# Second ConvGLU of a two-layer diffusion backbone in the seven-product scheme, with block sums made by adding transfers

## The chip, the cores and the metric

The kernel runs on one core of a Trainium2 chip. The metric is the device time of one execution in microseconds. Five engines work side by side, each through its own instruction stream in order: PE (TensorE: matmuls into PSUM, with weight loads listed apart as PEld), DVE (VectorE), ACT (ScalarE), POOL (GpSimd) and SP (SyncE, which only issues transfers). They wait for one another by semaphores. 16 DMA engines move the data.

## The reference

512 latent tokens and 256 context tokens of width 1024 pass two layers: attention and a ConvGLU (both streams), then a gated recurrence (HGRN2) and a ConvGLU (latent stream only). All is float32. What the change is about is the last part, the second ConvGLU:

```python
D_MODEL = 1024; SEQ = 512; D_FF = 2816; CONV_W = 3

def dwconv3(u, w, b):
    up = jnp.pad(u, ((0, 0), (1, 1), (0, 0)))
    return up[:, :-2] * w[0] + up[:, 1:-1] * w[1] + up[:, 2:] * w[2] + b

def conv_glu(h, w_up, conv_w, conv_b, w_down):
    gate, val = jnp.split(h @ w_up, 2, axis=-1)
    return (jax.nn.silu(dwconv3(gate, conv_w, conv_b)) * val) @ w_down

# in each layer
hx2 = rms_norm(x, norm2_g[layer]) * (1.0 + sc2) + sh2
x = x + g2 * conv_glu(hx2, ffn_w_up[layer], ffn_conv_w[layer], ffn_conv_b[layer], ffn_w_down[layer])
```

## The kernel before

Features lie on the 128 partitions, tokens along the free dimension. The program runs, in this order: norm and modulation, attention, its output projection (`attn_out`), the first ConvGLU (`ffn` with l=0, 770 columns: 512 latent, 256 context, two for the shifts), the recurrence (`hgrn`), its output projection (`hgrn_out`), the second ConvGLU (`ffn` with l=1, 514 columns), and the transposed output.

**Split operands.** A float32 factor x is split in two: ACT rounds it to wh, DVE makes wl = x - wh. A product is three matmuls: wh with the high and the low part of the activations, wl with the high part. A weight is first loaded raw by a transfer that SP issues (tile `wr`, pool `wp`, two buffers of 2048 columns), then split into operand tiles `wh`, `wl` of 512 columns, taken in turn from several small pools (`operand`). The splits carry a high priority, so they run ahead as far as buffers allow.

**ConvGLU.** `ffn` walks over 22 feature tiles `ft` of 128. `up(ft)` computes gate and value, runs the three-tap convolution, SiLU and the product on DVE and ACT, and keeps the split result `g`. After a round of tiles (`ROUNDS`), a down projection adds their part to the eight output tiles of x, one pair `dp` at a time. One tile of the next round is computed ahead of the down projection. The norm's factor R per token is applied to the output of the up projection, so it may come late; its row sums pass PE (`nss`), POOL (`rs`, the inverse root) and PE again (`nR`).

**Two forms of the up projection.** The first ConvGLU uses seven products (`load_pair`, `gate_pair`): the weights of a tile form a 2x2 matrix of blocks (a11, a12: first and second half of the 1024 inputs for the gate; a21, a22: the same for the value), the activations another (b11 to b22: input halves by column halves, made by `halves` and `combos` into the seven sets `hs`). Seven products of 4 k each with sums of blocks take the place of eight. DVE makes the four sums of weight blocks (L136) before the seven splits; POOL multiplies the value half by R. PSUM tiles pZ, pY and pV collect the products. ACT copies intermediate states of Z and V, DVE adds them. The second ConvGLU uses the plain form (`load_w`, `gate_plain`): four splits, 96 matmuls of 256 or 258 columns into `pd`, four evictions on DVE (L912). Its one set of split activations `hn` is made tile by tile in `hgrn_out` (`scaled`).

**What sets the order.** The code is written straight through; a list scheduler places each engine's instructions by priority and by its own estimate of readiness. The tile framework adds the semaphore waits. Each engine then runs its list in order.

## Time and profile before

| | us |
|---|---|
| three runs | 1875.34, 1877.10, 1877.72 (median 1877.1) |
| the profiled execution | 1872.88, span 1871.1 from first to last instruction |
| attention and its output projection | to about 428 |
| first ConvGLU | about 428 to 1003 |
| recurrence | about 1003 to 1412 |
| `hgrn_out` | about 1412 to 1481 |
| second ConvGLU and output | about 1481 to 1871 |

The stages are read from the first and last matmuls of each tile name. In rows of groups, `out<-in` names the tiles, then partitions x elements, the count after x, busy us and mean ns of one, and the idle time of the engine just before with what ended it. Clock is the TensorE clock that was granted, 1 being full.

### The profile page before, as it was taken

How to read it: one execution, taken by the hardware profiler on the slowest of the kernel's cores; microseconds unless marked ns; L12 is line 12 of the kernel's file. 1: busy time of each engine (PE TensorE's matmuls, PEld its weight loads, DVE VectorE, ACT ScalarE, POOL GpSimd, SP SyncE). 2: the span in 40 equal slices, each digit the busy share in tenths (PEclk: the TensorE clock that was granted, in tenths of full speed). 3: DMA queues.
4: the chain of work that ended last, by engine and by line, in shares of the span. 5: the costliest groups of instructions: out<-in, count | busy, mean ns of one | idle time of the engine just before them, and what ended most of it. 6: DMA issues, size and time to landing. Idle time of an engine off the chain costs nothing.

```text
span 1871.1 us, 32302 instructions
## 1 busy us (share of the span) xinstructions
PE 1801.3 (96%) x13326; PEld 1576.9 (84%) x13326; DVE 1214.1 (65%) x2243; ACT 754.7 (40%) x1478; POOL 247.4 (13%) x233
## 2 busy tenths in 40 slices
PE   6999999998999999999998999999998999999998
PEld 4976786787888888989887888988886799899997
DVE  5575667466867686766777676777676655455462
ACT  4354555465534252434354333333332443233332
POOL 1233333103201000101013101111110200000000
PEclk9999999998999999999998999999999999999999
DMA  9204104232333333233313212122220332333321
GB/s 309 66 23 158 47 24 169 68 102 68 124 113 102 113 124 113 91 113 124 113 61 90 58 35 58 35 57 58 57 69 24 90 91 91 90 96 96 92 82 65
DMA packets 204416, 166.44 MB, mean 89 GB/s; under 512 B 5149, under 2 KB 198254, under 8 KB 199150
## 3 DMA queue, kind: packets, MB, share of 16 engines
q1 hardware_dynamic: 196608, 160.47, 27.8%
q10 hardware_dynamic: 7662, 3.92, 0.7%
q8 instruction: 105, 1.72, 0.4%
q14 instruction: 41, 0.34, 0.1%
HBM read 162.27 MB, written 2.10 MB: 88 GB/s over the span
## 4 chain that ended last, share of the span: by engine, by line
PE 87%; DVE 5%; DMA 4%; issue 2%; ACT 1%; POOL 1%; SPq 0%; ACTq 0%; POOLq 0%; DVEq 0%
PE dn L170 15%; PE pd L170 13%; PE pZ L188 8%; PE pf L170 8%; PE pV L188 4%; PE pjq L598 4%; PE pv L170 4%; PE ao L170 4%; PE ho L170 3%; PE pq L170 3%; PE pv L824 2%; PE pt L816 2%; PE ada L309 2%; PE pY L188 2%; PE pgate L170 2%; PE kv L598 2%
## 5 line engine op out<-in xcount | busy, mean ns | idle before, releaser
L117 ACT ACTIVATE wh<-wr 128x512 fp32r<-128x512 f32 (+1 forms) x320 | 193.0, 618 | 452.3 <-DMA wr<-in_ffn_w_up 74.8
L118 DVE TENSOR_TENSOR wl<-wr,wh 128x512 fp32r<-128x512 f32 (+1 forms) x320 | 223.6, 705 | 140.3 <-ACT wh L117 138.3
L170 PE MATMUL dn<-g,wh 128*128 128x512 f32 (+1 forms) x1056 | 263.3, 357 | 2.2 <-ACT g L995 2.2
L170 PE MATMUL pd<-hn,wh 128*128 128x256 f32 (+1 forms) x1408 | 227.3, 284 | 0.9 <-issue 0.9
L170 PEld LDWEIGHTS dn<-g,wh 128*128 128x128 f32 x1056 | 175.4, 189 | 32.7 <-ACT g L995 2.8
L170 PEld LDWEIGHTS pd<-hn,wh 128*128 128x128 f32 x1408 | 194.2, 190 | 2.5 <-issue 2.3
L188 PE MATMUL pZ<-hs,wh 128*128 128x386 f32 x704 | 185.2, 345 | 3.0 <-ACT wh L140 1.5
L170 PE MATMUL dn<-g,wl 128*128 128x512 f32 (+1 forms) x528 | 159.4, 356 | 0.0
L140 ACT ACTIVATE wh<-wr 128x512 fp32r<-128x512 f32 x132 | 81.6, 628 | 167.9 <-DMA wr<-in_ffn_w_up 47.4
L170 PE MATMUL pd<-hn,wl 128*128 128x256 f32 x704 | 141.8, 283 | 0.0
L188 PEld LDWEIGHTS pZ<-hs,wh 128*128 128x128 f32 x704 | 128.0, 190 | 15.7 <-ACT wh L140 4.4
L141 DVE TENSOR_TENSOR wl<-wr,wh 128x512 fp32r<-128x512 f32 x132 | 94.0, 717 | 53.6 <-ACT wh L140 53.5
L170 PE MATMUL pf<-hn,wh 128*128 128x512 f32 (+1 forms) x512 | 119.3, 349 | 9.7 <-DVE xc L1023 8.8
L188 PE MATMUL pZ<-hs,wl 128*128 128x386 f32 x352 | 119.4, 343 | 2.2 <-DVE wl L141 2.2
L926 POOL TENSOR_TENSOR gg<-gg,R 128x772 f32<-128x772 f32 x22 | 53.9, 2449 | 458.3 <-DVE gg L925 446.6
L170 PEld LDWEIGHTS pd<-hn,wl 128*128 128x128 f32 x704 | 109.0, 190 | 0.0
L1023 DVE SCALAR_TENSOR_TENSOR xl<-dn,mod,xl 128x512 f32<-128x512 f32 x72 | 53.9, 748 | 73.7 <-PE dn L170 73.6
L170 PEld LDWEIGHTS dn<-g,wl 128*128 128x128 f32 x528 | 87.4, 188 | 14.8
L170 PEld LDWEIGHTS pf<-hn,wh 128*128 128x128 f32 x512 | 80.9, 192 | 22.5 <-ACT wh L117 9.1
L188 PE MATMUL pV<-hs,wh 128*128 128x386 f32 x352 | 92.2, 341 | 5.0 <-ACT hs L392 5.0
L598 PE MATMUL pjq<-wh,hn 128*128 128x256 f32 x384 | 77.8, 291 | 0.0
L188 PEld LDWEIGHTS pZ<-hs,wl 128*128 128x128 f32 x352 | 66.7, 190 | 6.6 <-DVE gg L925 3.4
(299 smaller groups left out, 3807.1 us busy)
## 6 DMA issues: line engine op xcount, KB each, us to landing
wr<-in_ffn_w_up SPq DMA_DIRECT2D x88, 512.0 KB, 5.1
wada<-in_ada_w SPq DMA_DIRECT2D x40, 1024.0 KB, 4.8
wr<-in_hgrn_w_in SPq DMA_DIRECT2D x40, 512.0 KB, 4.2
ar<-in_ada_w SPq DMA_DIRECT2D x32, 256.0 KB, 7.1
wr<-in_ffn_w_down SPq DMA_DIRECT2D x16, 512.0 KB, 4.1
wr<-in_ffn_w_down SPq DMA_DIRECT2D x8, 896.0 KB, 4.7
wr<-in_attn_w_in SPq DMA_DIRECT2D x6, 1024.0 KB, 8.1
wr<-in_attn_w_out SPq DMA_DIRECT2D x8, 512.0 KB, 4.9
```

What stands on the lines that cost most here:

```text
L117: nc.scalar.activation(wh, src, AF.Copy)
L118: nc.vector.tensor_tensor(wl, src, f(wh), op=ALU.subtract)
L140: nc.scalar.activation(ops[i][0], src, AF.Copy)
L141: nc.vector.tensor_tensor(ops[i][1], src, f(ops[i][0]), op=ALU.subtract)
L170: nc.tensor.matmul(o, lhsT=wt, rhs=at[:, t0:t0 + o.shape[1]], start=(first and n == 0 and i == 0), stop=(last and n == len(ks) - 1 and i = ...
L188: self.nc.tensor.matmul(ps, lhsT=wt, rhs=at, start=(first and k == 0 and i == 0), stop=(k == nk - 1 and i == 2), skip_group_check=not first)
L309: nc.tensor.matmul(ps[32 * j:32 * j + 32, 0:512], lhsT=self.cs[:, k, :], rhs=raw[:, j * 512:(j + 1) * 512], start=(k == 0), stop=(k == KT ...
L598: nc.tensor.matmul(out, lhsT=x, rhs=y[:, wk], start=(start and k == 0 and j == 0), stop=(stop and k == KT - 1 and j == 2))
L816: nc.tensor.transpose(pt[:, j * P:(j + 1) * P], pr[j][:, b * P:(b + 1) * P], self.ident)
L824: nc.tensor.matmul(pv[a * HD:(a + 1) * HD, 0:256], lhsT=V[:, tl, g, :], rhs=pT[:, a * 256:(a + 1) * 256], start=(b == 0), stop=(b == len(t ...
L926: times = lambda eng, o, x, y: eng.tensor_tensor(o, x, y, op=ALU.mult)
L1023: nc.vector.scalar_tensor_tensor(x[:, d], o, self.modc(l, v, 5, d), x[:, d], op0=ALU.mult, op1=ALU.add)
```

## The change

- **Blocks.** Raw weights are loaded in blocks of 512 columns (256 KB, one transfer each; `block`) from eight buffers, instead of 2048 columns from two. This concerns all weights and the conditioning matrix (`ada_steps`). Down weights come as 128 columns each instead of 256.
- **Seven products in the second ConvGLU.** `gate_plain` goes; `gate_pair` serves both. `hgrn_out` builds the seven sets by `halves` and `combos`; the last two of each set are made after all output tiles.
- **Sums by transfers.** For the second ConvGLU no engine makes the sums of weight blocks. Seven blocks are loaded per tile (some twice or three times), and POOL issues five transfers per tile from one block to another that add to what is there (L151 of the new program): first s1 += a22, s3 += a11, s4 += a11, then s2 += s1, s4 += s1. So that all sums are additions, signs move into `combos` (scale -1) and into `gate_pair` (copies with scale -1, subtractions). This sign change reaches the first ConvGLU too, whose sums stay on DVE.
- **Buffers.** A second pool of eight blocks (`wrB`) is opened for the second ConvGLU, 16 in all. The turn of operand pools changes to ten pairs there; `gpB` has 7 buffers for 9. R is multiplied on DVE instead of POOL there.
- **Rounds** of the second ConvGLU are 6, 6, 5, 5 for 8, 7, 7.

```diff
--- before.py
+++ after.py
...
-ROUNDS = ((3, 4, 4, 4, 3, 4), (8, 7, 7))
+ROUNDS = ((3, 4, 4, 4, 3, 4), (6, 6, 5, 5))
...
-    def load_raw(self, parts):
-        raw = self.wp.tile([P, 2048], F32, tag="wr", name="wr")
-        n = 0
+    def block(self, src):
+        nk, m = src.shape[1:]
+        pool = self.wps[0]
+        self.wps = self.wps[1:] + self.wps[:1]
+        raw = pool.tile([P, 512], F32, tag="wr", name="wr")[:, 0:nk * m]
+        self.nc.sync.dma_start(out=raw.rearrange("p (k m) -> p k m", m=m), in_=src)
+        return raw
+    def split(self, src, op=None):
+        wh, wl = op or (t[:, 0:src.shape[1]] for t in self.operand())
+        with self.tc.high_priority(offset=W_AHEAD):
+            self.nc.scalar.activation(wh, src, AF.Copy)
+            self.nc.vector.tensor_tensor(wl, src, f(wh), op=ALU.subtract)
+        return wh, wl
+    def load_w(self, parts):
+        out = []
         for src in parts:
             nk, m = src.shape[1:]
...
+            step = 512 // m
+            blocks = [self.block(src[:, k:min(k + step, nk)]) for k in range(0, nk, step)]
+            ops = [self.split(b) for b in blocks]
+            out += [ops[i:i + 2] for i in range(0, len(ops), 2)]
         return out
-    def load_pair(self, parts, tmp):
...
+    def load_pair(self, parts, tmp, lat_only):
+        nc = self.nc
+        p1, p2 = parts
+        low, high = slice(0, 4), slice(4, 8)
+        ops = [self.operand() for _ in range(7)]
+        def total(o, x, y):
+            nc.vector.tensor_tensor(o, x, y, op=ALU.add)
...
-        with self.tc.high_priority(offset=W_AHEAD):
-            parts(0, a11)
-            parts(1, a12)
-            total(s1, a21, a22, ALU.add)
-            s3 = total(a21, a11, a21, ALU.subtract)
-            s2 = total(a11, s1, a11, ALU.subtract)
-            parts(3, s2)
-            parts(6, s3)
-            parts(2, s1)
-            parts(5, a22)
-            s4 = total(a12, a12, s2, ALU.subtract)
-            parts(4, s4)
+        if not lat_only:
+            a11, a12, a21, a22 = (self.block(p[:, k]) for p in parts for k in (low, high))
+            s1 = tmp.tile([P, 512], F32, tag="s1", name="s1")
+            with self.tc.high_priority(offset=W_AHEAD):
+                self.split(a11, ops[0])
+                self.split(a12, ops[1])
+                total(s1, a21, a22)
+                s3 = total(a21, a11, a21)
+                s2 = total(a11, s1, a11)
+                for i, src in ((3, s2), (6, s3), (2, s1), (5, a22)):
+                    self.split(src, ops[i])
+                self.split(total(a12, a12, s2), ops[4])
+            return ops
+        a11, a22, s1, s3, a12, s2, s4 = (self.block(p[:, k]) for p, k in
+                                         ((p1, low), (p2, high), (p2, low), (p2, low), (p1, high), (p1, low), (p1, high)))
+        with self.tc.high_priority(offset=2 * W_AHEAD):
+            for o, x in ((s1, a22), (s3, a11), (s4, a11), (s2, s1), (s4, s1)):
+                nc.gpsimd.dma_start(out=o, in_=x, accum_op=ALU.add)
+        for i, src in ((0, a11), (1, a12), (3, s2), (6, s3), (2, s1), (5, a22), (4, s4)):
+            self.split(src, ops[i])
         return ops
...
-            raw = self.wp.tile([P, 2048], F32, tag="wr", name="wada")
-            nc.sync.dma_start(out=raw, in_=self.a["ada_w"][l, k * P:(k + 1) * P, r * 2048:(r + 1) * 2048])
+            raw = []
...
-                nc.tensor.matmul(ps[32 * j:32 * j + 32, 0:512], lhsT=self.cs[:, k, :], rhs=raw[:, j * 512:(j + 1) * 512],
+                raw.append(self.wp.tile([P, 512], F32, tag="wr", name="wada"))
+                nc.sync.dma_start(out=raw[j], in_=self.a["ada_w"][l, k * P:(k + 1) * P, r * 2048 + j * 512:r * 2048 + j * 512 + 512])
+            for j in range(4):
+                nc.tensor.matmul(ps[32 * j:32 * j + 32, 0:512], lhsT=self.cs[:, k, :], rhs=raw[j],
...
-        def put(i, src):
-            nc.scalar.activation(hs[i][:, 0, kk], src, AF.Copy)
-            nc.vector.tensor_tensor(hs[i][:, 1, kk], src, f(hs[i][:, 0, kk]), op=ALU.subtract)
+        def put(i, src, sign=1.0):
+            nc.scalar.activation(hs[i][:, 0, kk], src, AF.Copy, scale=sign)
+            if sign > 0:
+                nc.vector.tensor_tensor(hs[i][:, 1, kk], src, f(hs[i][:, 0, kk]), op=ALU.subtract)
+            else:
+                nc.vector.scalar_tensor_tensor(hs[i][:, 1, kk], src, sign, f(hs[i][:, 0, kk]), op0=ALU.mult, op1=ALU.subtract)
...
-            put(5, diff(b21, t4, t3))
+            put(5, diff(b21, t3, t4))
...
         put(0, b11)
...
         t1 = diff(b12, b12, b11)
-        put(2, t1)
+        put(2, t1, -1.0)
...
-        put(3, t2)
+        put(3, t2, -1.0)
...
-        put(5, diff(b21, b21, t2))
+        put(5, diff(b21, t2, b21))
...
-        if R.shape[1] > TW:
-            nc.vector.memset(R[:, TW:], sh)
+        if R.shape[1] > TW or lat_only:
+            nc.vector.memset(R[:, C0 if lat_only else TW:], sh)
...
-    def gate_plain(self, ft, ops, hn, G, gg, R, rows, half, tmp, bank):
...
-    def gate_pair(self, ft, ops, hs, G, gg, R, rows, half, tmp, bank):
...
+    def gate_pair(self, ft, ops, hs, G, gg, R, rows, lat_only, tmp, bank):
+        nc = self.nc
+        half = hs[0].shape[3]
...
+        less = lambda o, x: nc.vector.tensor_tensor(o, o, x, op=ALU.subtract)
...
         prod(0, Z, True)
...
         prod(1, Y, True)
         add(g[0], t0, Y)
         prod(3, Z)
-        nc.scalar.activation(g[2], Z, AF.Copy)
+        nc.scalar.activation(g[2], Z, AF.Copy, scale=-1.0)
...
         if ft == 0:
             prod(2, Z)
...
             prod(4, Z)
             prod(6, V, True)
-            nc.scalar.activation(g[3], V, AF.Copy)
+            nc.scalar.activation(g[3], V, AF.Copy, scale=-1.0)
             prod(5, V)
         else:
             prod(6, V, True)
-            nc.scalar.activation(g[3], V, AF.Copy)
+            nc.scalar.activation(g[3], V, AF.Copy, scale=-1.0)
             prod(2, Z)
             nc.scalar.activation(t2, Z, AF.Copy)
             prod(5, V)
             prod(4, Z)
-        add(g[3], g[3], t2)
-        add(g[2], g[2], V)
+        less(g[3], t2)
+        less(g[2], V)
...
         times(nc.vector, g[0], g[0], R[:, 0:half])
         times(nc.vector, g[1], Z, R[:, half:])
-        times(nc.gpsimd, gg, gg, R)
+        times(nc.vector if lat_only else nc.gpsimd, gg, gg, R)
...
-        half = C0 // 2 if lat_only else hs[0].shape[3]
+        half = hs[0].shape[3]
...
         def up(ft):
-            ws_ = [self.wcols(wup, ft * P, P), self.wcols(wup, DFF + ft * P, P)]
-            ops = self.load_w(ws_) if lat_only else self.load_pair(ws_, tmp)
+            ops = self.load_pair([self.wcols(wup, ft * P, P), self.wcols(wup, DFF + ft * P, P)], tmp, lat_only)
...
-            (self.gate_plain if lat_only else self.gate_pair)(ft, ops, hs, G, gg, R, rows, half, tmp, bank)
+            self.gate_pair(ft, ops, hs, G, gg, R, rows, lat_only, tmp, bank)
...
             for dp in range(KT // 2):
-                w = self.load_w([wdn[f0 * P:(f0 + nf) * P, dp * 256:dp * 256 + 256].rearrange("(k p) m -> p k m", p=P)], True)
+                w = self.load_w([wdn[f0 * P:(f0 + nf) * P, d * P:d * P + P].rearrange("(k p) m -> p k m", p=P)
+                                 for d in (2 * dp, 2 * dp + 1)])
...
-    def hgrn_out(self, part, hn, acc, tmp, pj):
-        nc = self.nc
-        self.shifts(1, 1, hn)
+    def hgrn_out(self, part, hs, acc, tmp, pj):
+        nc = self.nc
...
+        some = []
...
                 self.add_gated(1, 2, d, pd, True)
+            some.append(self.combos(self.halves(1, 1, dp, 258, True, tmp, ("y0", "y1"), 4), dp, hs))
+            next(some[-1])
...
-                self.scaled(1, 1, d, hn, True)
...
+        for rest in some:
+            for _ in rest:
+                pass
...
-        self.wp = self.pool(top, "wp", 2)
+        self.wp = self.pool(top, "wp", 8)
...
+        self.wps = [self.wp]
...
-        self.wsp.append(self.pool(top, "wsC", 2))
+        wsC = self.pool(top, "wsC", 2)
+        self.wsp = [self.ws0, wsC, self.ws0]
...
-        self.wsp.append(self.pool(top, "wsD", 2, right=True))
+        wsD = self.pool(top, "wsD", 2, right=True)
+        self.wsp = [self.ws0, wsC, self.ws0, wsD]
...
-        hn = self.hn_tile(hc, "hn3", C0)
+        hs1 = hc.tile([P, 7, 2, 4, 258], F32R, tag="hs", name="hs3")
+        hs = [hs1[:, i] for i in range(7)]
...
-        self.hgrn_out(part, hn, acc, ot, pj)
+        self.hgrn_out(part, hs, acc, ot, pj)
...
-        R = Rp.tile([P, C0], F32, tag="R", name="R2")
+        R = Rp.tile([P, 516], F32, tag="R", name="R2")
...
-        gp = self.pool(es, "gpB", 9)
-        self.wsp.append(self.pool(es, "wsE", 2))
+        gp = self.pool(es, "gpB", 7)
+        self.wps = [self.wp, self.pool(es, "wrB", 8)]
+        self.wsp = [self.ws0, wsC, self.ws0, wsD, self.pool(es, "wsE", 2)]
...
-        self.ffn(1, hn, R, rows, True, tmp, acp, bk, gp, done1)
+        self.ffn(1, hs, R, rows, True, tmp, acp, bk, gp, done1)
```

At the start of the second ConvGLU, POOL's list ended like this before (`acc2`: sum of squares for the norm; `rs`: inverse root; numbers tell buffers apart):

```order
L515 TENSOR_TENSOR acc2_15106<-acc2_15106,sq_15222 128x512 [waits Activation_49,Pool_49]
L515 TENSOR_TENSOR acc2_15106<-acc2_15106,sq_15297 128x512 [waits Activation_49,Pool_49]
L515 TENSOR_TENSOR acc2_15106<-acc2_15106,sq_15302 128x512 [waits Activation_49,Pool_49]
L429 TENSOR_TENSOR rs_15405<-rv_15406,mh_66 128x4 [waits DVE_49]
L1449 UNCONDITIONAL_BRANCH
```

and now (`wr<-wr`: an adding transfer; for the first tile a11 is 16000, a22 16002, s1 16004, s3 16006, a12 16008, s2 16010, s4 16012; 161xx is the second tile):

```order
L518 TENSOR_TENSOR acc2_15666<-acc2_15666,sq_15932 128x512 [waits Activation_49,Pool_49]
L432 TENSOR_TENSOR rs_16084<-rv_16085,mh_66 128x4 [waits DVE_49]
L151 DMA wr_16004<-wr_16002 128x512 [waits DMAHW0_49,DMAHW1_49,DVE_49,Pool_49]
L151 DMA wr_16006<-wr_16000 128x512 [waits DMAHW1_49]
L151 DMA wr_16182<-wr_16176 128x512 [waits DMAHW4_49,DMAHW3_49]
L151 DMA wr_16180<-wr_16178 128x512 [waits DMAHW4_49]
L151 DMA wr_16010<-wr_16004 128x512 [waits DMAHW2_49,DMASW1_49]
L151 DMA wr_16012<-wr_16004 128x512 [waits DMASW0_49]
```

The first tile's s1 and s3 come right behind `rs`; its second level (s2, s4) waits for transfers (DMASW) and stands behind two sums of the second tile.

SP's list at the same place before (raw weights of 512 KB a transfer):

```order
L95 DMA wr_15329<-in_ffn_w_up 128x8x128 [waits DMAHW6_49,DMAHW5_49,DVE_49]
L95 DMA wr_15329<-in_ffn_w_up 128x8x128
L95 DMA wr_15481<-in_ffn_w_up 128x8x128 [waits DMAHW7_49,DMAHW0_49,DVE_49]
L95 DMA wr_15481<-in_ffn_w_up 128x8x128
L95 DMA wr_15618<-in_ffn_w_up 128x8x128 [waits DMAHW2_49,DMAHW1_49,DVE_49]
```

and now:

```order
L96 DMA wr_16336<-in_ffn_w_up 128x4x128 [waits DMAHW6_49,DVE_49]
L96 DMA wr_16340<-in_ffn_w_up 128x4x128 [waits DMAHW7_49,DMAHW1_49,DVE_49]
L96 DMA wr_16002<-in_ffn_w_up 128x4x128 [waits DVE_49,DMAHW0_49,PE_49,Pool_49]
L96 DMA wr_16006<-in_ffn_w_up 128x4x128
L96 DMA wr_16010<-in_ffn_w_up 128x4x128 [waits DMAHW2_49]
L96 DMA wr_16176<-in_ffn_w_up 128x4x128 [waits DMAHW3_49]
```

The blocks from the new pool (16002, 16006, 16010 of the first tile) come behind two of the third tile, and the first of them waits for PE and POOL.

On PE the piece after the output projection read before:

```order
L170 MATMUL pd<-hn_15102,wl 128x256
L170 MATMUL pd<-hn_15102,wl 128x258
L524 MATMUL nss<-cst,acc_15106 128x2 x4
L533 MATMUL nR<-dg,cst 128x512
L170 MATMUL pd<-hn_15102,wh 128x256
```

and now:

```order
L186 MATMUL pY<-hs_15662,wh 128x258 x2
L186 MATMUL pY<-hs_15662,wl 128x258
L527 MATMUL nss<-cst,acc_15666 128x2 x4
L186 MATMUL pV<-hs_15662,wh 128x258 x2
L536 MATMUL nR<-dg,cst 128x512
L186 MATMUL pZ<-hs_15662,wh 128x258 x2
```

`nss` stood behind 48 matmuls of the first tile and now stands behind its products 0 and 1 (24 matmuls); two matmuls on a sum of weight blocks stand ahead of `nR`.

More of the change, by code (lines that the diff above doesn't have):

```diff
@@ L96, in load_raw @@
-            n += nk * m
-        return raw, n
-    def load_w(self, parts, cols=False):
-        nc = self.nc
-        raw, n = self.load_raw(parts)
-        nk, m = parts[0].shape[1:]
-        out = []
-        for lo in range(0, m, P) if cols else range(0, n, 1024):
-            size = nk * P if cols else min(1024, n - lo)
-            ops = []
-            for i in range(0, size, 512):
-                c = min(512, size - i)
-                wh, wl = (t[:, 0:c] for t in self.operand())
-                src = raw[:, lo + i:lo + i + c]
-                with self.tc.high_priority(offset=W_AHEAD):
-                    if cols:
-                        src = ap(raw[:, i // P * m + lo:i // P * m + lo + 1], 0, (m, c // P), (1, P))
-                        wh, wl = (t.rearrange("p (k c) -> p k c", c=P) for t in (wh, wl))
-                    nc.scalar.activation(wh, src, AF.Copy)
-                    nc.vector.tensor_tensor(wl, src, f(wh), op=ALU.subtract)
-                    if cols:
-                        wh, wl = (t.rearrange("p k c -> p (k c)") for t in (wh, wl))
-                ops.append((wh, wl))
-            out.append(ops)
-        return out
@@ L125, in load_pair @@
-    def load_pair(self, parts, tmp):
-        nc = self.nc
-        raw, n = self.load_raw(parts)
-        q = n // 4
-        a11, a12, a21, a22 = (raw[:, i * q:(i + 1) * q] for i in range(4))
-        s1 = tmp.tile([P, 512], F32, tag="s1", name="s1")[:, 0:q]
-        ops = [tuple(t[:, 0:q] for t in self.operand()) for _ in range(7)]
-        def total(o, x, y, op):
-            nc.vector.tensor_tensor(o, x, y, op=op)
-            return o
-        def parts(i, src):
-            nc.scalar.activation(ops[i][0], src, AF.Copy)
-            nc.vector.tensor_tensor(ops[i][1], src, f(ops[i][0]), op=ALU.subtract)
-        with self.tc.high_priority(offset=W_AHEAD):
-            parts(0, a11)
-            parts(1, a12)
-            total(s1, a21, a22, ALU.add)
-            s3 = total(a21, a11, a21, ALU.subtract)
-            s2 = total(a11, s1, a11, ALU.subtract)
-            parts(3, s2)
-            parts(6, s3)
-            parts(2, s1)
-            parts(5, a22)
-            s4 = total(a12, a12, s2, ALU.subtract)
-            parts(4, s4)
+            step = 512 // m
```

13 lines of the change are left out of this document (1 added, 12 removed).

## The prediction

> **What bounds the kernel now.** I read the page's busy times first, then the chain of waits, then a table by stage, then PE's waits.
>
> ```profile
> PE 1801.3 (96%) x13326; PEld 1576.9 (84%) x13326; DVE 1214.1 (65%) x2243; ACT 754.7 (40%) x1478; POOL 247.4 (13%) x233
> PE 87%; DVE 5%; DMA 4%; issue 2%; ACT 1%; POOL 1%; SPq 0%; ACTq 0%; POOLq 0%; DVEq 0%
> ```
>
> PE is busy nearly all the time, and it is also the chain. For the second ConvGLU, where most of the change lies, the chain in order of time reads:
>
> ```profile
> 1483.57 4.62 issue
> ...
> 1490.12 2.04 PE nR L533 x2
> 1492.16 98.39 PE pd L170 x816
> 1590.55 44.23 PE dn L170 x192
> 1634.78 80.50 PE pd L170 x672
> 1715.28 38.60 PE dn L170 x168
> 1753.88 69.00 PE pd L170 x576
> ```
>
> `pd` is the up projection, `dn` the down projection. From 1492 to 1823 us nothing but matmuls stands in the chain: this stage is bound by the number and width of matmuls. An up matmul costs 98.39/816 = 0.1206 us (256 or 258 columns), a down matmul 44.23/192 = 0.2304 us (512 columns). The table by stage gives the other engines (columns: PE, PEld, DVE, ACT, POOL busy us; clock; DMA share; GB/s), for an up stretch, a down stretch and the whole first ConvGLU:
>
> ```profile
> 1492.16:1590.55 98.39, 98.39 (x818) 98.39 (x817) 59.44 (x120) 40.13 (x62) 0.00 (x0) 0.99 0.29 87
> 1590.55:1634.78 44.23, 44.23 (x195) 36.13 (x194) 17.35 (x27) 10.48 (x18) 0.00 (x0) 1.00 0.33 95
> 428.00:1003.00 575.00, 553.57 (x3124) 496.58 (x3116) 419.77 (x697) 243.30 (x442) 80.31 (x48) 0.99 0.34 106
> ```
>
> The first ConvGLU already uses the seven products; there DVE is busy for 419.77/575 = 73% and PE hardly waits for the splits:
>
> ```profile
> PE pZ L188 <- DVE wl L141: 2.2, 3, 1.6
> PE pZ L188 <- ACT wh L140: 1.5, 4, 0.4
> ```
>
> **The products.** Before, a feature tile takes 2 outputs x 8 k x 3 x 2 column halves = 96 matmuls; after, 7 products x 4 k x 3 = 84 of 258 columns. Over 22 tiles 264 matmuls fall away: 264 x 0.1206 = 31.8 us. The price at exactly this width and with one use of each weight is not in the trace; the nearest row besides is the first ConvGLU's product of 386 columns:
>
> ```profile
> 646.60 2.13 PE pZ L188 x12
> ```
>
> That is 0.1775 us each. A line through it and the 512-column matmul gives 0.1238 at 258 columns, so the saving would be 2112 x 0.1206 - 1848 x 0.1238 = 25.9 us. I take 31.8, since `pd` has the same width; 25.9 is the lower end. The down matmuls stay (528 of 512 columns). Rounds of 6, 6, 5, 5 for 8, 7, 7 add eight evictions on DVE,
>
> ```profile
> L1023 DVE SCALAR_TENSOR_TENSOR xl<-dn,mod,xl 128x512 f32<-128x512 f32 x24 | 18.0, 750 | 48.1 <-PE dn L170 48.1
> ```
>
> 0.75 us each, under down stretches in which DVE is busy for 17.35 of 44.23 us: nothing.
>
> **DVE and ACT in an up stretch.** One tile must now fit under 84 x 0.1206 = 10.13 us of PE. The means of single instructions, second ConvGLU:
>
> ```profile
> L118 DVE TENSOR_TENSOR wl<-wr,wh 128x512 fp32r<-128x512 f32 x112 | 76.8, 687 | 70.5 <-ACT wh L117 70.3
> L989 DVE SCALAR_TENSOR_TENSOR u<-G,par,u 128x512 f32<-128x512 f32 x22 | 16.5, 752 | 0.8
> L992 DVE SCALAR_TENSOR_TENSOR gg<-gg,u 128x512 f32<-128x512 f32 x22 | 16.4, 747 | 0.0
> L996 DVE TENSOR_TENSOR g<-gg,g 128x512 fp32r<-128x512 f32 x22 | 15.2, 693 | 15.4 <-ACT g L995 15.4
> L912 DVE TENSOR_TENSOR G<-pd,R 128x258 f32<-128x258 f32 x22 | 9.2, 418 | 0.0
> L985 DVE TENSOR_SCALAR cb<-G,wsum,par 128x1 f32<-128x1 f32 x22 | 5.9, 267 | 0.0
> L983 DVE COPY G<-G 128x1 f32<-128x1 f32 x22 | 3.3, 149 | 0.0
> L117 ACT ACTIVATE wh<-wr 128x512 fp32r<-128x512 f32 x111 | 68.2, 630 | 159.4 <-DMA wr<-in_ffn_w_up 69.4 <-PE pd L170 37.2 <-PE dn L170 26.3
> ```
>
> DVE after: 7 splits x 0.687, five operations of 258 columns x 0.418, one of 516 at 0.69, two u at 0.75, then 0.747, 0.693, 0.267 and 0.149: 10.95 us. The same sum for today's tile (4 splits, four evictions, the same tail) is 7.78 us, or 66 us for the 8.5 tiles of the first up stretch, where DVE was really busy for 59.44: means overlap by a tenth. So 10.95 means about 9.9 busy, 97% of an up stretch. Over a whole round the down stretch gives relief (ten operand pairs let splits run ahead): 22 x 9.9 plus four times some 14 in the down stretches (8 evictions, 16 splits a round) is 80% of 222.9 + 121.6 us of PE, against the 73% that cost the first ConvGLU next to nothing. ACT goes from 4 to 7 splits (4.4 us) and gets four copies of 258 columns; its tail stays, so it keeps room. Bounds: 0 below, 22 x (10.95 - 10.13) = 18 above; I take 4, nearer to the first ConvGLU's rows.
>
> **The seam into the second ConvGLU.** `hgrn_out` now builds seven operand sets instead of one. Under the output matmuls there is room; exposed is what follows the last one. The rows of POOL, SP and PE shown with the change tell the rest. POOL had nothing behind `rs`; now the first tile's sums stand behind it, the second level waits for the first to land, and later tiles' sums are queued behind that wait. On SP the first tile's blocks from the new pool (16002, 16006, 16010) wait for PE, since the pool takes the place of buffers that the last output matmul reads, and the loads behind them wait too. The old seam:
>
> ```profile
> 1479.67 0.40 PE L170 MATMUL ho<-oh,wl 128*128 128x512 f32 x1
> 1480.96 0.72 PE L170 MATMUL pd<-hn,wh 128*128 128x256 f32 x4 [0.89 <-issue]
> ...
> 1486.77 0.95 PE L524 MATMUL nss<-cst,acc 128*128 128x2 f32 x8
> 1488.23 1.02 POOL L429 TENSOR_TENSOR rs<-rv,mh 128x4 f32<-128x4 f32 x1 [4.66 <-DVE rv L428]
> ```
>
> ```profile
> wr<-in_ffn_w_up SPq DMA_DIRECT2D x88, 512.0 KB, 5.1
> ar<-in_ada_w SPq DMA_DIRECT2D x32, 256.0 KB, 7.1
> xs<-in_x ACTq DMA_DIRECT2D x8, 256.0 KB, 2.7
> ```
>
> New: eviction 0.75, ACT's scaled copy, one split, so products 0 and 1 (24 matmuls, no sums) end near 1485; `nss` and `rs` until 1487.5; level one lands 2.7 later (a 256 KB transfer's lower row), level two 2.7 after that, split 0.63 + 0.69: 1494.2. By then today's kernel has done 48 + 17 matmuls, the new one 26: 39 x 0.1206 = 4.7 us lost. With 7.1 for each landing it is 13.5. I take 8, since all blocks of two tiles arrive at once there. If the loads were early, nothing but the 2 us before product 0 would show.
>
> **Transfers in the stage.** In finer blocks of 256 KB the same bytes move for the rest of the program; PE waits there for DMA only at the start (first row), so I count nothing. In the second ConvGLU a tile loads 7 blocks for 4 and makes 5 sums. Slices of 1.5 us from 1740 to 1800:
>
> ```profile
> PE ada L275 <- DMA ar<-in_ada_w: 10.8, 3, 9.0
> ...
> DMA  5000399000089400004982000079600000970000
> GB/s 126 0 0 0 89 330 270 20 0 0 9 253 323 114 0 0 0 0 119 265 240 86 0 5 0 0 215 330 165 0 0 0 0 27 307 277 0 0 11 0
> ```
>
> A full slice moves about 330 GB/s, so 7 + 2 blocks of 0.262 MB take 7.1 us. A sum moves at least two times 0.262 MB (1.6 us), at most three (2.4 us: two reads and a write, none overlapping): 7.9 to 11.9 us for five. PE needs 10.13 + 24 x 0.2304 = 15.7 us per tile; with 15.0 the transfers fit, with 19.0 not. I take the lower: reads and writes of one copy overlap in every load of this trace.
>
> The Trainium skill, "Collectives: The Full Stack", § The bandwidth ceiling, says that an add in the DMA path costs two source reads on one ring and therefore runs at half a copy's rate, not slower for the adding itself; by it an adding transfer takes twice a copy, the 1.6 us above, and no run here shows it yet.
>
> **Sum.** 1872.9 (profiled execution, span 1871.1 and 1.8 around it) - 31.8 + 4 + 8 = 1853.1. The median of the runs lies 4.2 us above the profiled one: 1857.
>
> **Rivals.**
> *All hidden* (15%): the seam costs 2 and DVE nothing: 1872.9 - 31.8 + 2 + 4.2 = 1847. For it: PE's few waits in the first ConvGLU. Against: the order of POOL above.
> *DVE paces the up stretches* (10%): 18 for the 4: 1871. For it: 97%; against: the 73% row.
> *The adding transfers pace it, slower* (20%): 19.0 us a tile for 15.7 is 22 x 3.3 = 73 us more: 1930. It decides from 1.7 us a sum on, and the gain is gone at 1.9. Against: a copy's overlap; for: nothing in this trace has ever added in flight.
> *POOL's issuing slows DVE* (5%): POOL and DVE do hinder one another here (start us, us).
>
> ```profile
> 1457.09 4.69 POOL L515 TENSOR_TENSOR acc<-acc,sq 128x512 f32<-128x512 f32 x3 [11.41 <-ACT sq L513]
> 1453.67 0.68 DVE L118 TENSOR_TENSOR wl<-wr,wh 128x512 fp32r<-128x512 f32 x1
> 1458.92 1.72 DVE L118 TENSOR_TENSOR wl<-wr,wh 128x512 fp32r<-128x512 f32 x1
> ```
>
> A split beside POOL's adds takes 1.72 us for 0.68. If each of 5 issues did that once, DVE had 9.9 + 5.2 a tile, and a round of six 6 x 15.1 + 15 = 106 us for PE's 94: 22 x 2 = 44 us more, 1901. The Trainium skill, "SBUF — State Buffer", § Who interferes with whom, infers the opposite for writing descriptors beside a tensor_tensor; only POOL operations that read SBUF hinder it. The rows above agree with the second half.
>
> **The numbers.** Forecast 50%, own range 1848 to 1867. Measurable is about 0.2% (3.8 us). Faster: 0.95 of the 50%, all of the 15%, half of the 10%: 67%. Slower: the 20 and 5% and an eighth of the 10%: 26%. Within: 7%. The range is 1843 to 1900: some 3% is left out below, and above some 17 of the slow 25%.
>
> **What would show it.** Right: products of 12 in about 1.45 us, up stretches of about 10.2 us a tile with PE unbroken, a hole of some 10 us after the last `ho`, sums landing in under 4 us, DMA share near 0.9 at most. Wrong: PE or ACT waiting for `wr` in the middle of an up stretch, DMA share at 1, splits longer than 0.75 us, or ACT's copies of Z late.

## The result and the profile after

The change is slower: 1928.7 us (median of 4 runs, 1926.2 to 1935.3) against 1876.8 us before, a ratio of 1.0283 with a 95% interval of 1.0254 to 1.0312. I had forecast 1857 us. The profiled execution of the change took 1935.3 us, with a span of 1933.5 us; it is the longest of the four, so losses read from its rows come out some us larger than those between medians.

Two rows of the page of the changed kernel, the busy times and the shares of the chain of waits:

```profile
PE 1829.7 (95%) x13062; PEld 1566.1 (81%) x13062; DVE 1299.9 (67%) x2412; ACT 829.9 (43%) x1682; POOL 344.6 (18%) x351
PE 82%; DMA 8%; DVE 5%; issue 2%; ACT 2%; POOL 1%; ACTq 0%; SPq 0%; POOLq 0%; DVEq 0%
```

PE issues 264 matmuls fewer and is busy 28 us longer. To see where, I took the first and last matmul of three stages: the attention's output (`ao`), the first one of `hgrn` (`pf`) and the output of `hgrn` (`ho`). First before, then the change (columns: shortest/median/longest ns, then first and last start in us):

```profile
L170 PE MATMUL ao<-oh,wh x256: 274/336/505, 348.4 to 425.6; 128*128 128x512 f32 x128
L170 PE MATMUL pf<-hn,wh x512: 276/389/763, 1003.8 to 1376.7; 128*128 128x512 f32 x86, 128*128 128x258 f32 x85
L170 PE MATMUL ho<-oh,wl x64: 391/396/629, 1413.1 to 1479.7; 128*128 128x512 f32 x64
```

```profile
L168 PE MATMUL ao<-oh,wh x256: 274/336/505, 363.6 to 439.0; 128*128 128x512 f32 x128
L168 PE MATMUL pf<-hn,wh x512: 276/389/763, 1028.7 to 1401.4; 128*128 128x512 f32 x86, 128*128 128x258 f32 x85
L168 PE MATMUL ho<-oh,wl x64: 390/394/632, 1437.4 to 1507.4; 128*128 128x512 f32 x64
```

The change is 15 us late when the attention's output begins, 25 us late at `hgrn`, and 28 us late at the last `ho`. So almost half of the 62 us by which the span grew lies ahead of the second ConvGLU. From the last `ho` to the end it takes 426.1 us for 391.4. That row of the table by stage, before and after (PE, PEld, DVE, ACT, POOL busy; clock; DMA share; GB/s):

```profile
1479.70:1871.10 391.40, 382.64 (x2684) 357.79 (x2682) 198.62 (x379) 129.35 (x206) 2.30 (x2) 0.99 0.29 87
```

```profile
1507.40:1933.50 426.10, 370.22 (x2420) 340.33 (x2418) 273.63 (x532) 196.43 (x390) 97.19 (x112) 0.93 0.82 189
```

DMA is at 0.82 for 0.29, and PE, idle for 9 us of this stage before, now is for 56, at a mean granted clock of 0.93 for 0.99. The chain of the change, in order of time, begins that stage with transfers where it had only matmuls:

```profile
1517.49 5.63 DMA wr<-in_ffn_w_up
1524.27 7.03 DMA wr<-wr
1531.59 7.57 DMA wr<-wr
1541.70 2.58 PE pZ L186 x12
...
1604.35 6.11 PE pZ L186 x36
...
1870.03 4.32 PE pZ L186 x36
```

`wr<-wr` is a sum of blocks. Two land one after the other, 7.0 and 7.6 us each, behind a load of 5.6. They end the third of three holes in PE's work after the last `ho`; the brackets give their lengths:

```profile
1510.20 0.48 PE L186 MATMUL pZ<-hs,wh 128*128 128x258 f32 x2 [2.37 <-DVE wsum L955]
1528.78 0.80 PE L186 MATMUL pV<-hs,wh 128*128 128x258 f32 x2 [14.50 <-ACT wh L103]
1540.90 0.80 PE L186 MATMUL pV<-hs,wh 128*128 128x258 f32 x2 [3.37 <-ACT wh L103]
```

Behind the third hole a matmul takes 2.58/12 = 0.215 us, and later 4.32/36 = 0.120 us. The granted clock is 0.50 for 4.0 us behind the hole of 14.5 us and for 5.5 us behind that of 3.4, and 1.00 behind that of 2.4. So the two longer holes are paid twice. The Trainium skill, "TensorE: Matmul & The Clock Gate", § Part 1: The HAM clock gate, says that an idle window of about 3.4 us halves PE's clock; these three holes agree. The waits in the second ConvGLU of the change (us, times, longest):

```profile
PE pV L186 <- ACT wh L103: 18.7, 3, 14.5
PE pZ L186 <- ACT t L935: 15.2, 5, 8.8
PE dn L168 <- ACT g L983: 5.1, 1, 5.1
...
ACT wh L103 <- DMA wr<-wr: 62.3, 17, 10.8
POOL wr L151 <- DMA wr<-wr: 81.6, 22, 6.1
POOL wr L151 <- DMA wr<-in_ffn_w_up: 58.3, 15, 24.5
```

ACT waits for the sums (62.3 us), and behind its waiting splits stand the copies of Z (`t`) that PE waits for: that is the sign "ACT's copies of Z late" which I had listed against myself.

### The profile page after: what moved, and what is told of

It is laid out like the page before. It is cut to its first block, busy times and chain, and to the rows that moved or that the text cites. A ratio compares the mean times of both kernels' runs of the same rounds, so it can differ in the third digit from the quotient of the medians.

```text
span 1933.5 us, 33878 instructions
## 1 busy us (share of the span) xinstructions
PE 1829.7 (95%) x13062; PEld 1566.1 (81%) x13062; DVE 1299.9 (67%) x2412; ACT 829.9 (43%) x1682; POOL 344.6 (18%) x351
## 4 chain that ended last, share of the span: by engine, by line
PE 82%; DMA 8%; DVE 5%; issue 2%; ACT 2%; POOL 1%; ACTq 0%; SPq 0%; POOLq 0%; DVEq 0%
PE dn L168 14%; PE pZ L186 13%; PE pf L168 7%; PE pV L186 7%; DMA wr<-wr 4%; PE ada L309 4%; PE pjq L601 4%; PE pv L168 4%; PE ao L168 4%; PE pY L186 3%; DMA wr<-in_ffn_w_up 3%; PE pgate L168 3%; PE pq L168 2%; PE pv L827 2%; PE pt L819 2%
## 5 line engine op out<-in xcount | busy, mean ns | idle before, releaser
L103 ACT ACTIVATE wh<-wr 128x512 fp32r<-128x512 f32 (+3 forms) x534 | 321.0, 609 | 646.9 <-PE pZ L186 156.8
L104 DVE TENSOR_TENSOR wl<-wr,wh 128x512 fp32r<-128x512 f32 (+3 forms) x534 | 371.4, 702 | 181.0 <-ACT wh L103 168.0
L186 PE MATMUL pZ<-hs,wh 128*128 128x386 f32 (+1 forms) x1408 | 325.0, 321 | 27.3 <-ACT t L935 15.2
L186 PEld LDWEIGHTS pZ<-hs,wh 128*128 128x128 f32 x1408 | 244.2, 196 | 55.1 <-ACT t L935 16.2
L186 PE MATMUL pZ<-hs,wl 128*128 128x386 f32 (+1 forms) x704 | 222.1, 318 | 0.0
L186 PE MATMUL pV<-hs,wh 128*128 128x386 f32 (+1 forms) x704 | 162.3, 318 | 21.4 <-ACT wh L103 18.7
L151 POOL DMA_DIRECT2D wr<-wr x110 | 95.8, 965 | 283.5 <-DMA wr<-wr 81.6
L186 PEld LDWEIGHTS pV<-hs,wh 128*128 128x128 f32 x704 | 121.9, 195 | 25.7 <-ACT wh L103 21.2
L186 PE MATMUL pV<-hs,wl 128*128 128x386 f32 (+1 forms) x352 | 111.0, 316 | 0.7 <-DVE wl L104 0.7
L309 PE MATMUL ada<-wada,cs 128*32 128x512 f32 x320 | 84.0, 604 | 1.9 <-DVE xc L898 1.4
```

The lines of the kernel that those rows point to most:

```text
L103: self.nc.scalar.activation(wh, src, AF.Copy)
L104: self.nc.vector.tensor_tensor(wl, src, f(wh), op=ALU.subtract)
L151: nc.gpsimd.dma_start(out=o, in_=x, accum_op=ALU.add)
L186: self.nc.tensor.matmul(ps, lhsT=wt, rhs=at, start=(first and k == 0 and i == 0), stop=(k == nk - 1 and i == 2), skip_group_check=not first)
L309: nc.tensor.matmul(ps[32 * j:32 * j + 32, 0:512], lhsT=self.cs[:, k, :], rhs=raw[j], start=(k == 0), stop=(k == KT - 1), tile_position=(0, ...
```

## The experiments

Two losses had to be explained: some 28 us ahead of the second ConvGLU, and in it about 66 us between the 31.8 that I had forecast as saved and the 34.7 lost. My theory for the first was the modulation rows, for the second the adding transfers, by their bytes or by their latency.

**The modulation matmuls.** The group of L309 (its last numbers: busy us, mean ns, idle before) in the kernel before, and in the change:

```profile
L309 PE MATMUL ada<-wada,cs 128*32 128x512 f32 x320 | 45.3, 604 | 3.4 <-DMA wada<-in_ada_w 1.9 <-DVE xc L895 1.4
```

```profile
L309 PE MATMUL ada<-wada,cs 128*32 128x512 f32 x320 | 84.0, 604 | 1.9 <-DVE xc L898 1.4
```

The same 320 instructions of the same 604 ns keep PE busy 38.7 us longer. PE's timeline shows how, before and after:

```profile
170.63 1.06 PE L309 MATMUL ada<-wada,cs 128*32 128x512 f32 x8
...
174.00 1.07 PE L309 MATMUL ada<-wada,cs 128*32 128x512 f32 x8
```

```profile
170.34 1.04 PE L309 MATMUL ada<-wada,cs 128*32 128x512 f32 x2
171.32 0.38 PE L775 MATMUL S<-KA,qT 128*128 128x256 f32 x1
...
172.13 1.05 PE L309 MATMUL ada<-wada,cs 128*32 128x512 f32 x2
173.11 0.66 PE L819 MATMUL pt<-cst,Pc 128*128 128x128 f32 x4
173.69 1.05 PE L309 MATMUL ada<-wada,cs 128*32 128x512 f32 x4
```

The four matmuls of a row (two records each) use four different strips of 32 columns of the array and run at the same time: eight records in 1.06 us. Two alone take 1.04. In the change each waits for its own block, so the scheduler puts a ready matmul of another kind between them, and a row costs two or three times 1.05 us. The Trainium skill, "TensorE: Matmul & The Clock Gate", § Part 3: Packing small matmuls — row/col tiling, gives the span of such a pack as one matmul plus some 4 ns for each further one; these rows agree, 1.04 against 1.06.

*ada_last_first*: the four are written so that the one that waits longest goes first.

```diff
-            for j in range(4):
+            for j in reversed(range(4)):
                 nc.tensor.matmul(ps[32 * j:32 * j + 32, 0:512], ...
```

> The change with one thing altered: the four modulation matmuls of a row of ada_w (L309) are written in the order 3, 2, 1, 0, so that the first one waits for the block that lands last and the other three follow it without another engine's work between. Theory A (the groups of four fell apart): in the trace of the change those 320 instructions keep PE busy for 84.0 us against 45.3 before, in groups that take 1.05 us whether they hold 2 or 8 instructions, and the second ConvGLU begins about 25 us late. Then this run gives PE about 45 to 50 us for L309 back, and a time of about 1928.7 - 25 = 1904 us. Rival B (finer loads): the 25 us come from four times as many loads and waits in blocks of 512 columns; then L309 gets shorter, but the time stays within 5 us of 1929.

Measured 1901.0 us, 27.7 less. Its row of L309 (what stands behind the bar is again busy us, mean ns and idle time before):

```profile
L309 PE MATMUL ada<-wada,cs 128*32 128x512 f32 x320 | 47.0, 613 | 10.3 <-DMA wada<-in_ada_w 8.9 <-DVE xc L898 1.4
```

The blocks are still small; only the order in the group changed. PE is busy 37.0 us less on these matmuls and waits 8.9 us for their blocks instead of 0.5, which leaves 28.6. Rival B falls.

*before_ada_four*: the old kernel with that one thing.

```diff
-            nc.sync.dma_start(out=raw, in_=...[..., r * 2048:(r + 1) * 2048])
+            for j in range(4):
+                nc.sync.dma_start(out=raw[:, j * 512:(j + 1) * 512], in_=...)
```

> The kernel before with one thing altered: a row of ada_w comes into the same 2048-column buffer by four transfers of 512 columns for one; everything else keeps its large blocks. Theory A: the matmuls of L309 fall apart here too (PE busy about 80 us for 45.3), and the time rises from 1876.8 to about 1895 to 1902 us. Rival B: only a whole kernel of small blocks is slow, so the time stays at 1877 within 5 us.

Measured 1919.5 us, 44 more than before, with L309 at 80.7 us. The direction is as theory A has it, the size is above it. Over the whole kernel PE is busy 37.5 us longer (1838.8 for 1801.3) and waits 6.4 us for these blocks instead of 1.9. Why the 38.7 us of the change made it only 28 us late was not followed.

**The adding transfers.** A tile's seven loads are three blocks twice and one block once; none comes three times. The change's two rows on them, the queue of POOL's transfers (packets, MB, share of 16 engines over the span) and the issues (KB, median us to landing):

```profile
q0 software_dynamic: 15840, 28.84, 8.7%
...
wr<-wr POOLq DMA_DIRECT2D x110, 256.0 KB, 6.4
```

One sum thus takes 0.087 x 1933.5/110 = 1.53 us of all 16 engines.

*no_sums*: none of the five.

```diff
-            for o, x in ((s1, a22), (s3, a11), (s4, a11), (s2, s1), (s4, s1)):
+            for o, x in ():
```

> The change without its 110 adding transfers: the seven blocks of a tile are still loaded and split, but the sums of blocks are left out, so the products are taken of unsummed blocks and the output isn't the reference's. Theories S1 (the adding transfers fill the DMA engines) and S2 (their latency, two in a row behind a load, holds the block buffers): the second ConvGLU falls from 426 us to about 360 (348 us of PE work and a seam of 10), so about 1863 us. Rival S3 (seven splits a tile on DVE and ACT pace it): nothing of that changes, so the time stays at 1915 us or above.

Measured 1883.3 us, 45.5 less; the stage took 375.5 us. S3 falls: seven splits a tile are still there.

```profile
1508.60:1884.10 375.50, 355.78 (x2420) 328.56 (x2418) 275.07 (x531) 199.74 (x389) 2.96 (x3) 0.97 0.48 137
```

Of the 50.6 us that the stage lost to the sums, 14.4 are the same 2420 matmuls at a lower clock (370.22 for 355.78 busy, clock 0.93 for 0.97), the rest is idle time. The loads alone take 0.48 x 375.5 us of the engines for 137 GB/s x 375.5 us = 51.4 MB, which is 0.92 us a block, where I had taken 0.79.

*ada_no_sums*: both at once.

> Both repairs of the change at once: the modulation matmuls in the order 3, 2, 1, 0, and no adding transfers (the sums of blocks are left out, so the output isn't the reference's). If the two losses are apart and are all that my sum lacked, they add: 1928.7 - 27.7 - 45.4 = 1855.6 us, within 4 us, which is also what my sum gave with these two at nothing (1857). If they overlap (a part of the one hides a part of the other), it stays above 1862 us.

Measured 1855.1 us: the two losses add to within 1 us. That the rest agrees with my sum to 2 us is in part luck, as shown below. PE's waits from the last `ho` on in that run:

```profile
PE pV L186 <- ACT wh L103: 6.2, 1, 6.2
PE dn L168 <- ACT g L983: 5.1, 1, 5.1
PE pZ L186 <- DVE wsum L955: 3.0, 1, 3.0
PE xo L1404 <- DVE xl L1012: 0.7, 2, 0.4
```

*flat_sums*: as many transfers and bytes, but the second level adds a loaded block.

```diff
-            ... (s4, a11), (s2, s1), (s4, s1)):
+            ... (s4, a11), (s2, a22), (s4, a22)):
```

> The change with the same 110 adding transfers and the same bytes, but one level deep: the second-level sums add the loaded block a22 where they added the sum s1, so no sum needs another block's sum (the sums s2 and s4 are then not the reference's, and neither is the output). s4 still takes two sums in a row. S1, bytes on the DMA engines: the time stays within 6 us of 1928.7, and the DMA share in the up stretches stays near 0.97. S2, the latency of two levels and POOL's wait between them (81.6 us for sums): most of that wait goes, and the time falls by 20 to 40 us, to 1890 to 1910.

Measured 1921.3 us, 7.4 less than the change, just outside what S1 allowed and far from S2's 20 to 40. But the edit did not take away what it was meant to: s4 still takes two sums in a row, and POOL waits as long for landings as in the change (81.6 us there). ACT waits less than its 62.3 us there:

```profile
POOL wr L151 <- DMA wr<-wr: 83.4, 18, 7.1
ACT wh L103 <- DMA wr<-wr: 41.2, 12, 10.3
```

So this run shows only that it matters little whether the second level adds a sum or a loaded block. It does not rule out latency.

*half_sums* (on ada_last_first, 1901.0 us, as are the next four):

```diff
-                nc.gpsimd.dma_start(out=o, in_=x, accum_op=ALU.add)
+                nc.gpsimd.dma_start(out=o[:, 0:256], in_=x[:, 0:256], accum_op=ALU.add)
```

> The repaired change (modulation matmuls in the order 3, 2, 1, 0, 1901.0 us) with the same 110 adding transfers, each over 256 of the 512 columns: half the bytes, the same number of transfers, levels and waits (the other half of each sum is left out, so the output isn't the reference's). Leaving all sums out took the second ConvGLU from 426.1 to 375.5 us. S1 (bytes in the DMA engines): about half of these 50 us come back, 1901 - 25 = 1876 us. S2 (a fixed time from issue to landing, two in a row, and POOL's waits in order): it stays above 1892 us.

Measured 1874.9 us, 26.1 less, as S1 has it. But the landing fell too, from 6.3 us in ada_last_first to 4.4, so this alone does not part bytes from latency:

```profile
q0 software_dynamic: 15840, 14.42, 5.3%
...
wr<-wr POOLq DMA_DIRECT2D x110, 128.0 KB, 4.4
```

Half the bytes cost 0.053 x 1869.5/110 = 0.90 us for 1.53.

*first_tile_early*:

```diff
-        self.wps = [self.wp, self.pool(es, "wrB", 8)]
+        self.wps, self.wrB = [self.wp], self.pool(es, "wrB", 8)
...
+            if lat_only and ft == 1:
+                self.wps = [self.wp, self.wrB]
```

> The repaired change with the first feature tile's seven blocks all taken from the old pool of eight buffers; the new pool, which takes the place of buffers that the last output matmul reads, is used from the second tile on. The loads of the first tile and its first sums then run under the last output matmuls. If the seam is what I think (PE waits 2.4 us before product 0 and 14.5 us before the first product of a sum, at a granted clock of 0.72 afterwards), 14 to 20 us come back: about 1884 us. If the transfers pace the stage behind it anyhow and only the later tiles' sums are waited for, it stays within 5 us of 1901.

Measured 1888.2 us, 12.8 less, a little under the 14 to 20 expected. PE's longest wait for a split falls from 14.2 us (ada_last_first) to 5.1, and the transfers behind it do not eat the gain up.

*six_rounds*: `ROUNDS[1]` is (3, 3, 4, 4, 4, 4).

> The repaired change (1901.0 us) with rounds of 3, 3, 4, 4, 4, 4 tiles for 6, 6, 5, 5: the same products, loads and sums, 16 more evictions on DVE. Theory P (the peak): a tile's seven loads at 0.92 us and five sums at 1.54 us take 14.1 us of the DMA engines, in an up stretch PE wants a tile every 10.1 us, and the 16 buffers let only about 2.3 tiles a round be brought in under a down stretch; so (22 - 4 x 2.3) x 4.0 = 51 us are lost now, and (22 - 6 x 2.3) x 4.0 = 33 us with six rounds: about 18 us less and some 2 us more at the end, where a round of 4 hides less of the last tile's tail: 1885 us. Theory M (the mean): 8.9 blocks x 0.92 + 5 x 1.54 = 15.9 us a tile against PE's 15.7 over up and down together sets the time; rounds change nothing: 1901 to 1905 us.

Measured 1888.8 us, 12.3 less. The mean theory M falls; P's sign is right.

*fewer_buffers*: four buffers in the new pool, used for every third block.

> The repaired change with 12 block buffers for 16 (four in the new pool, every third block). Theory P: 1.7 tiles a round can be ahead for 2.3, (22 - 4 x 1.7) x 4.0 = 61 us for 51: about 1911 us. Theory M: within 5 us of 1901. If the landing times (two sums in a row, 5 to 8 us each) hold the buffers, a third fewer of them cost much more, 1930 us.

Measured 1938.3 us, 37.3 more: neither P's 10 nor M's nothing, but near the third guess, that the landing times hold the buffers. SP, which issues the loads, waits 145.8 us for landed sums in this stage, and 79.2 in ada_last_first. P's formula falls as a price.

*more_buffers*: 20, on six_rounds.

```diff
-        gp = self.pool(es, "gpB", 7)
-        self.wps = [self.wp, self.pool(es, "wrB", 8)]
+        gp = self.pool(es, "gpB", 5)
+        wrB = self.pool(es, "wrB", 12)
+        self.wps = [self.wp, wrB, self.wp, wrB, wrB]
```

> The run with rounds of 3, 3, 4, 4, 4, 4 (1888.8 us) with 20 block buffers for 16; the room comes from two buffers of g that rounds of four don't need. 12 for 16 buffers cost 37 us. If what limits the stage is how long a tile's seven blocks stay held (load, one or two sums, split: some 22 us, times 7 blocks, over 16 buffers is a tile every 10 us, over 12 every 13), 20 buffers give a tile every 8 us, under PE's 10.1: 15 us or more come back, to 1874 us or less. If the bytes limit it, the earlier loads only queue longer, the DMA share goes to 0.9 and the time stays within 5 us of 1889.

Measured 1889.2 us against 1888.8: nothing. So with these rounds it is, from 16 buffers on, no longer their number (the two `g` buffers that made room are not missed, or hide a small gain).

*aside_sums*: the same transfers into buffers that nothing reads, on six_rounds.

```diff
-            for o, x in ((s1, a22), (s3, a11), (s4, a11), (s2, s1), (s4, s1)):
+            for n, x in enumerate((a22, a11, a11, s1, s1)):
+                o = self.aside[(self.turn + n) % 4]
```

> The run with rounds of 3, 3, 4, 4, 4, 4 (1888.8 us) with the same 110 adding transfers of the same size from the same blocks, but into four buffers set aside, that nothing reads: the splits take the unsummed blocks as soon as they are loaded, and only a block that a transfer still reads is held longer (the products are of unsummed blocks, so the output isn't the reference's). If the bytes in the DMA engines set the pace, the time stays within 6 us of 1889. If it is the time that a split waits for landings in a row, with its block held, it falls to what leaving the sums out gives: 1883.3 - 27.7 = 1856 us, and a few us more for the sources that stay held: 1856 to 1866.

Measured 1875.0 us, 13.7 less: between the two theories. A 60 us window from the middle of the stage, of six_rounds and then of aside_sums:

```profile
1641.20:1701.20 60.00, 57.80 (x391) 53.27 (x391) 46.27 (x87) 31.30 (x60) 16.09 (x19) 1.00 1.01 234
```

```profile
1638.10:1698.10 60.00, 60.00 (x413) 55.80 (x412) 47.11 (x89) 31.76 (x60) 17.42 (x20) 1.00 1.08 253
```

The engines are full in both (this share adds up packets that overlap and can pass 1). With the waits for sums gone PE is no longer idle there, although the same bytes move. Over the five such windows in the middle of the stage PE is idle for 4.8 us against 16.2; in the 40 us behind the last `ho` it is 15.1 against 20.5, so a part of the gain is the seam's. My reading is that the bytes alone just about keep up with PE here, and that each wait on top of them is lost time, since full engines cannot catch up. That is argued and not shown: blocks are also held for a shorter time in this run, and POOL's order of issue, in which a later tile's sums stand behind a wait, was not tried by itself.

**Versions without the loss.** *ada_one_level*: two sums in flight, two on DVE, five loads a tile.

```diff
+            for o, x in ((s1, a22), (s3, a11)):
+                nc.gpsimd.dma_start(out=o, in_=x, accum_op=ALU.add)
...
+            s2 = total(a11, a11, s1)
...
+            self.split(total(a12, a12, s2), ops[4])
```

> The repaired change with two adding transfers a tile for five and five loads for seven: s1 and s3 are added in flight, s2 and s4 by DVE (2 x 0.69 us a tile more). S1: a tile then takes about 5 + 2 loads of 0.93 us and 2 sums of 1.5 us, 9.5 us of the DMA engines for PE's 15.7, so the stage comes to 375 to 380 us as without sums: about 1855 us. S2 (latency): one landing is left in the chain, perhaps half of the 50 us comes back: 1875. S3 (DVE paces, now with 12.3 us of means a tile): no better than 1885.

Measured 1867.9 us (ratio to before 0.9957, 0.9941 to 0.9974), between S1's 1855 and S2's 1875. *ada_dve_sums*: four loads and all five sums on DVE, as in the first ConvGLU (`if not lat_only:` becomes `if True:`, six new buffers for eight).

> The repaired change with no adding transfer: the second ConvGLU makes its five sums on DVE as the first one does, from four loads (six buffers in the new pool for eight). S1 and S2 lose their cause; DVE gets 5 x 0.69 = 3.4 us a tile more, 14.4 us of means, about 13.0 busy, which over 22 tiles with 56 us in the down stretches is 342 us for PE's 344: if PE hardly feels that, about 1855 us; if DVE paces the up stretches (13.0 for PE's 10.1 us a tile), 1880 us or more.

Measured 1866.9 us (0.9952, 0.9936 to 0.9967), between the two guesses. Then both with the first tile's blocks early and rounds of 5, 5, 6, 6:

> Two adding transfers a tile and two sums on DVE (1867.9 us), with two things more: the first tile's blocks from the old pool, and rounds of 5, 5, 6, 6. In that run's trace PE waits 14.6 us before the first product of a sum and 2.6 us before product 0, and 5.2 us for the last tile's g before the last round's matmuls. If these waits are all that is left, the first goes by 10 to 13 us (12.8 where it was done alone) and the last by 2 to 3: about 1853 us. If the DVE sums pace it, or if hgrn_out gets longer by the earlier splits, 1862 us or more.

Measured 1860.4 us, ratio 0.9915 (0.9901 to 0.9928): the fastest kernel of this study with the whole computation in it. It missed its 1853: the seam still holds two short waits and the tail's wait hardly moved.

```profile
PE dn L173 <- ACT g L990: 4.4, 1, 4.4
PE pV L191 <- ACT wh L103: 4.2, 1, 4.2
PE pZ L191 <- DVE wsum L960: 4.1, 1, 4.1
```

> All five sums on DVE, no adding transfer (1866.9 us), with the same two things: first tile's blocks from the old pool, rounds of 5, 5, 6, 6. In that run's trace PE waits 7.4 us for the first tile's split, 2.1 us before product 0 and 4.9 us for the last tile's g. These are shorter than with transfers, so about 8 us come back: 1859 us. If DVE (320.99 us busy of the stage's 385.2) paces it once the holes are gone, 1865 us.

Measured 1868.6 us, no gain over 1866.9 and above both guesses: with DVE busy for 320 of the stage's 389.6 us a new wait of 10.0 us for ACT's copy `gg` took the place of the old ones. It was not followed further.

## Why the prediction was wrong

**The finer blocks elsewhere: nothing.** This step failed by 27.7 us. I wrote that the same bytes move and that PE waits for DMA only at the start. The bytes hold, and for these rows PE waited 1.9 us for DMA before and 0.5 us in the change. But the cut also made four waits of one, and so changed the order of PE's instructions. In that order, four or eight modulation matmuls stand in a row 35 times before, and 12 times in the change, which has 38 single ones. The prediction looked at that order around the second ConvGLU alone.

**The transfers: 15.0 against 15.7 us a tile, no cost.** This step failed by 45.5 us, though its price of a sum came near: 1.53 us for 1.6. That is in part luck, since the 1.6 is twice a load that I had too low at 0.79; a sum took 1.7 times a load of the stage without sums. The Trainium skill, "Collectives: The Full Stack", § The bandwidth ceiling, has an add at half a copy's rate; 1.7 is near that and below it. The term that was mis-sized is the loads, 0.92 us a block for 0.79, so 8.9 x 0.92 + 5 x 1.53 = 15.8 us a tile. I had taken 330 GB/s from the fullest slices between 1740 and 1800 us; the same view has this row of the loads' queue (packets, MB, share of 16 engines):

```profile
q1 hardware_dynamic: 9616, 5.30, 30.4%
```

That is 0.304 x 60 us for 5.30 MB, or 0.90 us a block of 0.262 MB. With it my own sum, 9 x 0.90 + 5 x 1.6, would have been 16.1 us for PE's 15.7, and by my own rule the transfers would not have fit. My reason for the lower price of a sum, that reads and writes of a copy overlap "in every load of this trace", is one that no row shows, since the rows don't tell reads from writes. It was also wrong to make a yes or no of it: "with 15.0 the transfers fit", and "It decides from 1.7 us a sum on". At 0.95 to 1.01 of PE's pace, nothing that is lost is won back. By the runs, early first blocks gave back 12.8 us and six rounds 12.3, each by itself; on six rounds, taking the splits' waits away at the same bytes gave another 13.7. The 19.9 us between that (1875.0) and no sums at all (1855.1, with the old rounds) I can't part into bytes and blocks held as sources; by the rows of the stage, 8.0 us of it are longer PE busy time (363.92 for 355.91) and the rest is idle time.

**The products: -31.8.** Right: 0.120 us a matmul at full clock, as taken, and not the 0.1238 of the lower end. In ada_no_sums PE's busy time in the stage fell by 382.64 - 355.91 = 26.7 us only, at a clock of 0.97 for 0.99.

**DVE and ACT: +4.** It was nothing: in ada_no_sums PE waits for no split between the seam and the end. My count of DVE's work (22 x 9.9 + 56 = 274 us) was met by 273.63, and ACT kept room.

**The seam: +8, from 4.7 to 13.5.** Too low for the change as it is. I took a sum's landing as 2.7 to 7.1 us; the two in the chain took 7.0 and 7.6. I let POOL's first sums start right behind `rs`; POOL waited 3.17 us more there for the first tile's load. And I had no lower clock: PE waits 2.4, 14.5 and 3.4 us and runs at half the clock behind the two longer holes. In the first 33.7 us after the last `ho` it works for 13.63 us, and without sums for 24.36:

```profile
1508.00:1541.70 33.70, 13.63 (x85) 12.22 (x86) 15.05 (x32) 11.89 (x25) 12.59 (x14) 0.72 0.78 180
```

```profile
1508.00:1541.70 33.70, 24.36 (x174) 22.62 (x173) 26.20 (x52) 19.80 (x39) 3.56 (x3) 0.85 0.76 194
```

The order of POOL and SP that I described, with the first tile's blocks from the new pool stuck behind the last output matmul, is what was seen; moving them gave the 12.8 us above.

**The rounds: nothing.** Off by about 5 us: PE waits 5.1 us for the last tile's `g`, and no such wait stands in this stage of the profile before. The last round now has four tiles of matmuls to hide that tail for six, and the tail of the seven products may be longer; which of the two weighs more was not tried (a last round of six had 4.4).

**The sum.** With the two failed terms taken out on the chip, the kernel takes 1855.1 us where my sum said 1857; that they are so near is in part luck. In spans, the second ConvGLU fell from 391.4 to 375.5, by 15.9 us for my 19.8: 26.7 us less of PE's work for 31.8, and 10.8 us more of idle time (5.1 of it the tail, the rest the seam) for the 12 that I had put on seam and DVE. So the stage came out 3.9 us worse than my sum. Against that, the last `ho` starts 1.6 us earlier than before (1478.1 for 1479.7), and the 4.2 us that I added from the profiled run to the median were not there: this kernel's median lies 0.3 us below its profiled run.

**The rivals.** "The adding transfers pace it, slower" gave 1930 us, and the chip 1928.7, but not for its reason alone: it had 73 us for the transfers, which cost 45. The other 28 were in no case of mine, so the nearness of 1930 is luck. Of its signs, ACT waiting for `wr` and a DMA share of 1 came. "POOL's issuing slows DVE" is refuted: 184 full splits beside 109 issues take 686 ns as before (687), which is what the Trainium skill, "SBUF — State Buffer", § Who interferes with whom, infers for writing descriptors.

```profile
L104 DVE TENSOR_TENSOR wl<-wr,wh 128x512 fp32r<-128x512 f32 x184 | 124.6, 686 | 96.1 <-ACT wh L103 94.6 <-DMA wr<-in_ffn_w_up 0.9
L151 POOL DMA_DIRECT2D wr<-wr x109 | 94.8, 964 | 251.3 <-DMA wr<-wr 81.6 <-DMA wr<-in_ffn_w_up 58.3 <-DVE wl L104 31.7
```

## What to carry to other kernels

Before costing a smaller transfer by its bytes, look at who waits for the pieces: instructions that ran together because one wait released them may be pulled apart, and the order listing of the waiting engine shows it without a run. Price a transfer by its share of the engines over a stretch, and not by the fullest slice: here that alone moved the sum from 15.0 to 16.1 us a tile, across PE's 15.7. Where a resource's demand comes that near to the pace of the engine that it feeds, don't treat it as hidden: in this kernel the holes stayed, and PE's lower clock behind the longer ones came on top. Sums that DVE, with room left, makes in 0.7 us each were not better off in transfers that take 6 us to land.
